# The first output projection of a two-layer decoder kernel, turned from weight blocks to token tiles

## The chip, the cores and the metric

The kernel runs on one core of a Trainium2 chip. The metric is the device time of one execution in microseconds; the median of the runs shown is compared. The engines are named as in the profile: PE (matrix products, with its weight loads as PEld), DVE (vector), ACT (scalar, which also issues the stores), POOL, and SP (which issues the loads).

## The reference

Two layers over 1024 tokens of width 1024, batch 1. Each normalises its input, projects it, mixes tokens (layer A: dilated sliding-window attention in three groups of eight heads, merged per head; layer B: a gated linear recurrence), attends in four more heads to 256 memory rows, gates and projects back:

```python
h = rms_norm(x, norm_gain[l])
cols = h @ w_in                        # mixer | memory queries | gate
y = concat(mix, mem_out) * silu(gate)  # width 1024 + 512
x = x + y @ w_out                      # 1536 x 1024
```

The change concerns the last line of layer A and what stands before and after it.

## The kernel before

All matrix products keep single precision by splitting each operand into a high part and a remainder, and adding three products (high x high, high x remainder, remainder x high). A weight piece is 256 x 512 numbers, stored as 128 rows of 1024. `piece` (L189) loads it into one of two `raw` buffers (SP, L195), copies the high part `wh` (ACT, L166) and subtracts to get `wl` (DVE, L210). The pieces stand in one list in order of use; `take` (L233) hands out the next ones and `ahead(n)` (L227) makes sure that the next n are under way. They live in a ring of four slots (`wring`), which `more_weights` (L182) widens for a stretch by slots on the right-hand side of on-chip memory.

`project_tiles` (L256) takes four pieces, a 1024 x 512 block of weights, and goes over the eight token tiles of 128 in pairs. A pair sums into two of the three PSUM banks named `acc`, 2 x 24 matmuls of 128 x 512, and `each(m, ps)` empties a bank. The normalised input stands transposed and split on chip (`hhi`, `hlo`).

Layer A ends so. For the last head group the keys, values and queries are projected (L927 to L930). Each query tile goes through a norm, a rotary turn on POOL, a transposition, and `attend` (L834) for the tile before: scores, softmax, product with the values, and `merge` (L813), which reads the other two groups' outputs from DRAM into the two `os` buffers of the pool `gs` (`fetch_group`, L808), scales and adds them (L827, L830) and stores the tile to `o_scr`. The eighth tile's `attend` is called inside the last gate chunk (`gate_chunk`, L500), after its first pair of token tiles (L513). That chunk is the second half of the mixer's gate: per tile a tanh on ACT (L497), a product on DVE (L498) and a store to `gate_scr` (L512). Tiles 0 to 3 are written into the heads' `qn` buffers (`room`, L505), the others into `os`.

Then `out_proj` (L561) does the projection with `load_a` to `finish_a` (L949 to L982). Its steps run over three blocks `b0` of 512 rows of `w_out` (8: the memory heads, 0 and 4: the two halves of the mixer), and inside each over eight token tiles. A step loads a mixed slice and its gate (`ol`, `gt`, three buffers each, L955 or L957 and L958), multiplies them (L967), brings the product into transposed, split form (for b0 = 8 by a copy and a subtraction, L971 and L972; otherwise through four transpositions on PE, L291), and adds 2 x 12 matmuls (L609 to L611) into a pair of `acc` banks, which DVE adds to the input row `x1` (L616). Loads are issued three steps ahead and products made two steps ahead (`LEAD`). All eight `x1` tiles stay on chip. In the last block each tile is finished: stored, normalised (`norm_rows`, L272) and, one step later, transposed into the next layer's `hhi`, `hlo` (`put_hT`, L454). The weights come through the ring, widened by `W_OA` = 3 to seven slots. The first projection of layer B (L1002) follows.

What the program writes is not the order in which an engine works. The tile framework plans each engine's order ahead of the run, with expected times; what is written earlier goes first if it is ready. The engines then work through their planned order, and a buffer, on chip or in PSUM, passes to its next user when the last one is done with it. Pools that are closed give their memory to the pools opened next.

Of the kernel before, what the change touches and what calls it, by code (L numbers as in the profile page):

```python
# [30 lines left out]
D = 1024  # L31
# [16 lines left out]
LEAD = 2  # L48
# [2 lines left out]
ZR = 4  # L51
ZQ = 2
WR = 4
W_A, W_OA, W_B, W_OB = 1, 3, 2, 2
XL = 1
SQB = 1
MGP = ((0,),(1,),(),())
# [60 lines left out]
def trunk_kernel(ctx, tc, x, mem, pos, norm_gain, w_in_a, q_gain_a, k_gain_a, qk_gain_t, w_out_a,  # L118
# [58 lines left out]


    plan, ready = [], {}
    more, turn = [], [0]  # L180

    def more_weights(stack, n=2, start=0):  # L182

# [5 lines left out]
    def piece(src, gain=None):  # L189


        a = src.shape[1]
        raw = rpool.tile([128, 1024], F32, name="raw")
        v = lambda t: t.rearrange("p (a b) -> p a b", a=a)
        WQ.dma_start(v(raw[:]), src)  # L195
        pool = wpool
        if more:
# [12 lines left out]
        W_LO.tensor_tensor(lo[:], raw[:], hi[:].bitcast(F32), op=OP.subtract)  # L210
        return v(hi[:]), v(lo[:])
# [41 lines left out]
            if after:  # L253
                after(i)

    def project_tiles(key, lhs, each, order=None):  # L256

        W = take(key, 4)
        for m0 in range(0, NT, 2):
            pss = [pp.tile([128, 512], F32, name="acc") for _ in range(2)]  # L260
            project([ps[:] for ps in pss], [lhs(m0), lhs(m0 + 1)], W,
                    (lambda i: ahead(3 + i)) if m0 == NT - 2 else None, order)
            if m0 == 0:
                ahead(2)
            for i, ps in enumerate(pss):
                each(m0 + i, ps[:])
# [2 lines left out]
        copy(e_hi, hi, ps)  # L269
        V.tensor_sub(lo, ps, hi.bitcast(F32))  # L270

    def norm_rows(xt, gain, n, pool, parts=1):  # L272

        xn = pool.tile([128, D], F32, name="xn", bufs=2)
        ss = small.tile([128, 1], F32, name="ss1")
        A.activation(xn[:], xt, AF.Square, accum_out=ss[:])
        r = rsqrt(ss[:], 1, D)
        w = n // parts
        if gain is None:
            V.tensor_scalar(xn[:], xt, r[:], None, op0=OP.mult)  # L280
            return xn
        for c in (slice(i * w, (i + 1) * w) for i in range(parts)):
            V.scalar_tensor_tensor(xn[:, c], xt[:, c], r[:], gain[:, c], op0=OP.mult, op1=OP.mult)
        return xn
# [212 lines left out]
        A.activation(dst, src, AF.Tanh, scale=0.5)  # L497
        V.scalar_tensor_tensor(dst, dst, 1.0, src, op0=OP.add, op1=OP.mult)  # L498

    def gate_chunk(c, by_residue, between=None, room=None):  # L500

        def each(m, ps):
            pool, name = room if room and m < 4 else (gs, "os")  # L505
            sg = pool.tile([128, 4, 128], F32, name=name)[:].rearrange("p h d -> p (h d)")
            twice_silu(sg, ps)
            scr = gate_scr[:, c * 512:(c + 1) * 512]
# [3 lines left out]
                SQ.dma_start(sequence_rows(scr, m), sg)  # L512
            if between and m == 1:  # L513
                between()

        project_tiles(("gate", c), lhs_natural, each)

    def feature_proj(key, halves=lambda t, hf: t[:, hf * 512:(hf + 1) * 512]):

# [41 lines left out]
    def out_proj(key, load, load_x, y_T, x1, finish, pool, before):  # L561

        steps = [(b0, m) for b0 in FIRST for m in range(NT)]
        loaded, made, W = {}, {}, {}

        def weights(b0):
            p = take((key, b0), 4)
            W[b0] = [p[0:2], p[2:4]]  # L570

        def fetch(i):
            if i < len(steps):
                loaded[i], last = load(steps[i][1], steps[i][0])
                if XL <= i < NT + XL:
                    with tc.issue_after(last.ins):
                        load_x(i - XL)

        def make(i):
            if i < len(steps):  # L580
# [2 lines left out]
                y_T(steps[i][1], steps[i][0], loaded.pop(i), hi, lo)  # L583
                made[i] = hi, lo

        for i in range(LEAD + 1):
            fetch(i)
        for i in range(LEAD):
            make(i)
        before()  # L590
        later = None
        for i, (b0, m) in enumerate(steps):
            if m == 0:
                weights(b0)
            fetch(i + LEAD + 1)
            make(i + LEAD)
            if later:
                later()
                later = None
            hi, lo = made.pop(i)  # L600
            if m == 1:
                ahead(2)
            pss = [pp.tile([128, 512], F32, name="acc") for _ in range(2)]
            last = i == len(steps) - 1 and key == "out_b"
            for kp, ch in ((0, 0), (1, 0), (0, 1), (1, 1)) if last else ((0, 0), (0, 1), (1, 0), (1, 1)):
                wh, wl = W[b0][kp][ch]
                for j in range(2):
                    k = 2 * kp + j
                    T.matmul(pss[ch][:], hi[:, k, :], wh[:, j, :], start=k == 0, stop=False)  # L609
                    T.matmul(pss[ch][:], hi[:, k, :], wl[:, j, :], start=False, stop=False)  # L610
                    T.matmul(pss[ch][:], lo[:, k, :], wh[:, j, :], start=False, stop=k == 3)  # L611
                if m == NT - 1:
                    ahead(3 + 2 * kp + ch)
            for ch, ps in enumerate(pss):
                xs = x1[m][:, ch * 512:(ch + 1) * 512]
                V.tensor_tensor(xs, xs, ps[:], op=OP.add)  # L616
            if b0 == FIRST[-1]:
                later = finish(m)
        if later:
            later()  # L620


    gate_order = (8, 9), (10, 11, 0, 1, 2, 3, 4), (5, 6, 7)
# [47 lines left out]
    plan_out("out_b", w_out_b)  # L671

    wide = ExitStack()


    with ExitStack() as sa:
# [107 lines left out]
        with ExitStack() as s1:  # L784
# [103 lines left out]
            for Q, g in group_order:  # L888
# [39 lines left out]
                project_tiles(("v", Q, g), lhs, each_v, order)  # L928
                waiting = []
                project_tiles(("q", Q, g), lhs, each_q, order)  # L930
                last = lambda: attend(Q, g, *waiting.pop(), kT, kl, vv)
                if (Q, g) == group_order[-1]:
                    wide.close()
                    gate_chunk(1, False, last, (ap_, "qn"))
                else:
                    last()

    with ExitStack() as s2:  # L940
        more_weights(s2, W_OA, at_piece[1] - at_piece[0])
        op = s2.enter_context(tc.tile_pool(name="outp", bufs=1))
        x1 = op.tile([128, NT, D], F32, name="x1")
        x1 = [x1[:, m, :] for m in range(NT)]
        gainb = op.tile([128, D], F32, name="gainb")
        row_bcast(gainb[:], norm_gain[1], D)
        hnew = []

        def load_a(m, b0):  # L949
            r = slice(m * 128, (m + 1) * 128)  # L950
            o = op.tile([128, 512], F32, name="ol", bufs=3)
            gt = op.tile([128, 512], F32, name="gt", bufs=3)
            if b0 == 8:
                for t, scr in ((o, om_scr), (gt, gatem_scr)):
                    last = LQ.dma_start(t[:].rearrange("p (k t) -> p k t", k=4), scr[:, r].rearrange("(k p) t -> p k t", p=128))  # L955
            else:
                LQ.dma_start(o[:], o_scr[r, 0, b0 * 128:b0 * 128 + 512])  # L957
                last = LQ.dma_start(gt[:], gate_scr[r, b0 * 128:b0 * 128 + 512])  # L958
            return (o, gt), last

        def load_x(m):
            LQ.dma_start(x1[m], x[m * 128:(m + 1) * 128, :])

        def y_a(m, b0, loaded, hi, lo):
            o, gt = loaded
            y = o[:]
            V.tensor_tensor(y, y, gt[:], op=OP.mult)  # L967
            if b0 == 8:
                y = y.rearrange("p (k r j) -> p k j r", k=4, r=4)
                hi, lo = (t[:].rearrange("p k (j r) -> p k j r", r=4) for t in (hi, lo))  # L970
                copy(A, hi, y)  # L971
                V.tensor_sub(lo, y, hi.bitcast(F32))  # L972
                return
            transposed_split(y, hi, lo, 4)

        def finish_a(m):
            if not hnew:
                hnew.append(1)
                new_hT()
            xn = norm_rows(x1[m], gainb[:], D, op, 2 if m == NT - 1 else 1)  # L980
            SQ.dma_start(x1_scr[m * 128:(m + 1) * 128, :], x1[m])
            return lambda: put_hT(xn, m)  # L982

        out_proj("out_a", load_a, load_x, y_a, x1, finish_a, op, lambda: None)


    with ExitStack() as sb:
        more_weights(wide, W_B)
# [257 lines left out]
        with ExitStack() as s7:  # L1246
# [45 lines left out]
            out_proj("out_b", load_b, load_x, y_b, x1, finish_b, op, last_gates)  # L1292


# [40 lines left out]
```

## Time and profile before

| what | us |
|---|---|
| median of 3 runs (2157.15 to 2159.2) | 2158.18 |
| the profiled execution | 2157.36 |
| its span, first to last instruction | 2155.2 |
| PE busy | 2134.3 |
| DVE busy | 1079.5 |
| ACT busy | 729.8 |

Times in the views are from the start of the span. The chain of waits names who waited, for whom, in total, how often, and the longest; an entry in brackets in the timeline is idle time just before the instruction and what ended it. A row of a timeline gives start, length, engine, line, operation, output and inputs; an engine's name with a q is its queue issuing a transfer.

### The profile page before, as it was taken

What the parts mean: (1) busy time and instruction counts of PE and PEld (TensorE: products, weight loads), DVE (VectorE), ACT (ScalarE), POOL (GpSimd) and SP (SyncE); (2) the same over time, 40 slices, a digit from 0 to 9 for tenths busy, and PEclk for the clock granted to TensorE, in tenths of its full rate; (3) what the DMA queues carried; (4) which work ended last, traced back from release to release, by engine and by line L of the source; (5) the groups of instructions that cost most, each with busy time, mean ns of one, the idle gap of its engine ahead of it and who ended that gap; (6) DMA issues with size and microseconds to landing.
All of it is one profiled execution on the core that took longest, in us unless ns stands there. A gap on an engine that the chain in (4) does not pass through costs nothing.

```text
span 2155.2 us, 29643 instructions
## 1 busy us (share of the span) xinstructions
PE 2134.3 (99%) x11273; PEld 1813.5 (84%) x11273; DVE 1079.5 (50%) x2435; ACT 729.8 (34%) x1507; POOL 370.9 (17%) x600
## 2 busy tenths in 40 slices
PE   8999999999999999999999999999999999999999
PEld 6888888888888888888888877778888888888887
DVE  6755323324414324425834755634657772776443
ACT  4545323324423324323423521333532221232211
POOL 1013212312403302312222100012200000000221
PEclk9999999999999999999999999999999999999999
DMA  6543211221121121111311474420301112113633
GB/s 200 135 144 66 53 44 53 62 59 49 51 77 50 43 62 47 50 57 52 114 54 55 129 263 147 146 83 25 115 28 55 59 55 59 49 54 94 234 120 114
DMA packets 181004, 183.49 MB, mean 85 GB/s; under 512 B 49008, under 2 KB 117760, under 8 KB 180864
## 3 DMA queue, kind: packets, MB, share of 16 engines
q1 hardware_dynamic: 116592, 138.48, 21.2%
q10 hardware_dynamic: 64272, 43.13, 7.0%
q8 instruction: 89, 1.46, 0.3%
q14 instruction: 51, 0.42, 0.1%
HBM read 138.45 MB, written 43.12 MB: 84 GB/s over the span
## 4 chain that ended last, share of the span: by engine, by line
PE 95%; DMA 2%; DVE 1%; ACT 1%; issue 0%; SPq 0%; POOL 0%; ACTq 0%; DVEq 0%
PE acc L250 17%; PE acc L251 17%; PE acc L252 17%; PE acc L527 5%; PE acc L528 5%; PE acc L529 5%; PE acc L609 4%; PE acc L611 4%; PE acc L610 4%; PE po L877 3%; PE pt L308 2%; PE s L858 2%; PE s L1091 1%; PE pt L1091 1%; PE pt L871 1%; PE pt L291 1%
## 5 line engine op out<-in xcount | busy, mean ns | idle before, releaser
L250 PE MATMUL acc<-wh,hhi 128*128 128x512 f32 x1440 | 564.3, 395 | 2.4 <-ACT vb L166 1.2
L251 PE MATMUL acc<-wl,hhi 128*128 128x512 f32 x1440 | 566.1, 394 | 0.0
L252 PE MATMUL acc<-wh,hlo 128*128 128x512 f32 x1440 | 566.1, 395 | 0.0
L175 POOL TENSOR_TENSOR rr<-rv,nhalf 128x4 f32<-128x4 f32 (+1 forms) x150 | 147.5, 983 | 1374.3 <-DVE rv L173 1360.3
L210 DVE TENSOR_TENSOR wl<-raw,wh 128x1024 fp32r<-128x1024 f32 x152 | 189.0, 1244 | 368.0 <-ACT wh L166 365.9
L250 PEld LDWEIGHTS acc<-wh,hhi 128*128 128x128 f32 x1440 | 271.3, 188 | 56.0 <-ACT vb L166 1.4
L251 PEld LDWEIGHTS acc<-wl,hhi 128*128 128x128 f32 x1440 | 271.2, 188 | 53.2 <-DVE wl L210 0.4
L252 PEld LDWEIGHTS acc<-wh,hlo 128*128 128x128 f32 x1440 | 270.9, 188 | 53.0
L166 ACT ACTIVATE wh<-raw 128x1024 fp32r<-128x1024 f32 x152 | 160.7, 1059 | 186.1 <-PE acc L252 63.2
L529 PE MATMUL acc<-hhi,wl 128*128 128x512 f32 x512 | 204.1, 399 | 0.0
L528 PE MATMUL acc<-hlo,wh 128*128 128x512 f32 x512 | 203.8, 398 | 0.0
L527 PE MATMUL acc<-hhi,wh 128*128 128x512 f32 x512 | 203.0, 396 | 0.0
L609 PE MATMUL acc<-wh,yhi 128*128 128x512 f32 x384 | 152.8, 402 | 4.4 <-ACT yhi L166 2.6
L299 DVE TENSOR_REDUCE ss<-sq 128x4 f32<-128x512 f32 x116 | 79.3, 683 | 146.7 <-ACT sq L297 146.5
L610 PE MATMUL acc<-wl,yhi 128*128 128x512 f32 x384 | 151.1, 393 | 0.1
L611 PE MATMUL acc<-wh,ylo 128*128 128x512 f32 x384 | 149.4, 394 | 0.2 <-DVE ylo L972 0.2
L297 ACT ACTIVATE sq<-acc 128x512 f32<-128x512 f32 x116 | 68.9, 594 | 183.6 <-PE acc L252 179.5
L302 DVE TENSOR_TENSOR qn<-acc,rr 128x512 f32<-128x512 f32 x116 | 79.6, 688 | 92.9 <-PE pt L308 50.6
L866 ACT ACTIVATE pa<-pa,st 128x128 f32<-128x128 f32 (+1 forms) x192 | 84.4, 441 | 100.1 <-DVE st L864 96.0
L528 PEld LDWEIGHTS acc<-hlo,wh 128*128 128x128 f32 x512 | 96.4, 188 | 17.9
L527 PEld LDWEIGHTS acc<-hhi,wh 128*128 128x128 f32 x512 | 96.4, 188 | 17.6
L529 PEld LDWEIGHTS acc<-hhi,wl 128*128 128x128 f32 x512 | 96.4, 188 | 17.5
(233 smaller groups left out, 3191.7 us busy)
## 6 DMA issues: line engine op xcount, KB each, us to landing
raw<-in_w_in_a_dram SPq DMA_DIRECT2D x88, 512.0 KB
raw<-in_w_in_b_dram SPq DMA_DIRECT2D x40, 512.0 KB
o_scr<-os ACTq DMA_DIRECT2D x48, 256.0 KB
raw<-in_w_mem_kv_dram SPq DMA_DIRECT2D x16, 512.0 KB
os<-o_scr SPq DMA_DIRECT2D x32, 256.0 KB
raw<-in_w_out_a_dram SPq DMA_DIRECT2D x12, 512.0 KB
raw<-in_w_out_b_dram SPq DMA_DIRECT2D x12, 512.0 KB
gt<-gateb_scr SPq DMA_DIRECT2D x24, 256.0 KB
```

What stands on the lines that cost most here:

```text
L166: A.activation(dst, src, AF.Copy)
L175: G.tensor_tensor(r[:], v[:], nhalf[:, :n], op=OP.pow)
L210: W_LO.tensor_tensor(lo[:], raw[:], hi[:].bitcast(F32), op=OP.subtract)
L250: T.matmul(ps, hi, wh[:, j, :], start=at == 0, stop=False)
L251: T.matmul(ps, hi, wl[:, j, :], start=False, stop=False)
L252: T.matmul(ps, lo, wh[:, j, :], start=False, stop=at == n - 1)
L527: T.matmul(to, wh[:, k, :], mh, start=k == 0, stop=False)
L528: T.matmul(to, wh[:, k, :], ml, start=False, stop=False)
L529: T.matmul(to, wl[:, k, :], mh, start=False, stop=k == 7)
L609: T.matmul(pss[ch][:], hi[:, k, :], wh[:, j, :], start=k == 0, stop=False)
L610: T.matmul(pss[ch][:], hi[:, k, :], wl[:, j, :], start=False, stop=False)
L611: T.matmul(pss[ch][:], lo[:, k, :], wh[:, j, :], start=False, stop=k == 3)
```

## The change

**The order of the projection.** The steps run over token tiles, and inside a tile over the three blocks. The sum over all 1536 rows stays in one pair of `acc` banks, emptied once for each tile instead of three times. Each tile is finished at its third step.

```diff
-        steps = [(b0, m) for b0 in FIRST for m in range(NT)]
+        steps = [(b0, m) for m in range(NT) for b0 in FIRST] if by_tile else [(b0, m) for b0 in FIRST for m in range(NT)]
...
+                first, end = (b0 == FIRST[0], b0 == FIRST[-1]) if by_tile else (True, True)
+                if first:
+                    pss = [pp.tile([128, 512], F32, name="acc") for _ in range(2)]
...
+                        T.matmul(pss[ch][:], hi[:, k, :], wh[:, j, :], start=first and k == 0, stop=False)
...
+                for ch, ps in enumerate(pss) if end else ():
```

**Weights.** All twelve pieces have a place of their own (`W_OA` = 6): two in the widened ring, three in a pool over the last keys (`wearly`), three in a pool over the heads' buffers (`wlate`), four in the ring. A list `rooms` says which pool each piece goes to, for the first ten pieces of layer B too.

```diff
+        early, late = (s2.enter_context(tc.tile_pool(name=n, bufs=3, side="right")) for n in ("wearly", "wlate"))
+        rooms.extend([more[0]] * W_B + [early] * 3 + [late] * 3 + [wpool] * WR)
+        rooms.extend([more[0]] * W_B + [wpool] * WR + [more[0]] * W_B + [wpool] * (WR - W_B))
```

**When.** The pools are opened inside the last gate chunk, right after the eighth tile's `attend`, where those of the heads are closed. From gate tile 2 on the pieces are asked for two more at a tile, up to eight; the rest follow in the last pair. In that pair, after its first weight piece, the loads and products of the first two projection steps are made (`begin`); the rest of the projection (`rest`) comes after the chunk.

```diff
+            if between and m > 1:
+                ahead(min(W_OA + W_B, 2 * m - 2))
...
+                    def between():
+                        last()
+                        s1.close()
+                        sa.close()
+                        out_a.append(begin_out_a(s2))
+
+                    def to_out(i):
+                        if i == 0:
+                            out_a[0][0]()
+                        ahead(W_OA + W_B + 1 + i)
+
+                    gate_chunk(1, False, between, (ap_, "qn"), to_out)
```

**What pays for the memory.** The ring has four slots instead of five from the last queries on (`wide.close()` moves ahead of them, and `ahead` there asks for no more than four). `x1` has two buffers instead of eight tiles, `xn` one instead of two, `ol` two instead of three, and `gt` uses the two `os` buffers instead of three of its own. Gate tiles 2 and 3 go to `os` as well.

```diff
-            pool, name = room if room and m < 4 else (gs, "os")
+            pool, name = room if room and m < 2 else (gs, "os")
...
-            o = op.tile([128, 512], F32, name="ol", bufs=3)
-            gt = op.tile([128, 512], F32, name="gt", bufs=3)
+            o = op.tile([128, 512], F32, name="ol", bufs=2)
+            gt = gs.tile([128, 4, 128], F32, name="os")[:].rearrange("p h d -> p (h d)")
```

The load of `x1` for a tile is issued behind the loads of its third step. The second output projection (layer B) keeps its order.

More of the change, by code (lines that the diff above doesn't have):

```diff
@@ L179, in trunk_kernel @@
     plan, ready = [], {}
-    more, turn = [], [0]
+    more, turn, rooms = [], [0], []
     def more_weights(stack, n=2, start=0):
@@ L196, in piece @@
         pool = wpool
-        if more:
+        if rooms:
+            pool = rooms.pop(0)
+        elif more:
             if turn[0] >= WR:
@@ L254, in project, with project_tiles @@
                 after(i)
-    def project_tiles(key, lhs, each, order=None):
+    def project_tiles(key, lhs, each, order=None, end=None):
         W = take(key, 4)
@@ L261, in project_tiles @@
             project([ps[:] for ps in pss], [lhs(m0), lhs(m0 + 1)], W,
-                    (lambda i: ahead(3 + i)) if m0 == NT - 2 else None, order)
-            if m0 == 0:
+                    (end or (lambda i: ahead(3 + i))) if m0 == NT - 2 else None, order)
+            if m0 == 0 and not end:
                 ahead(2)
@@ L498, in twice_silu, with gate_chunk @@
         V.scalar_tensor_tensor(dst, dst, 1.0, src, op0=OP.add, op1=OP.mult)
-    def gate_chunk(c, by_residue, between=None, room=None):
+    def gate_chunk(c, by_residue, between=None, room=None, end=None):
         def each(m, ps):
-            pool, name = room if room and m < 4 else (gs, "os")
+            pool, name = room if room and m < 2 else (gs, "os")
             sg = pool.tile([128, 4, 128], F32, name=name)[:].rearrange("p h d -> p (h d)")
@@ L514, in each @@
                 between()
-        project_tiles(("gate", c), lhs_natural, each)
+            if between and m > 1:
+                ahead(min(W_OA + W_B, 2 * m - 2))
+        project_tiles(("gate", c), lhs_natural, each, end=end)
     def feature_proj(key, halves=lambda t, hf: t[:, hf * 512:(hf + 1) * 512]):
@@ L574, in fetch @@
                 loaded[i], last = load(steps[i][1], steps[i][0])
-                if XL <= i < NT + XL:
+                xm = i // 3 if by_tile and i % 3 == 2 else i - XL if not by_tile and XL <= i < NT + XL else None
+                if xm is not None:
                     with tc.issue_after(last.ins):
-                        load_x(i - XL)
+                        load_x(xm)
         def make(i):
@@ L584, in make, with begin @@
                 made[i] = hi, lo
[L586 to L596, printed above, removed]
+        def begin():
+            for i in range(LEAD):
+                fetch(i)
+            for i in range(LEAD):
+                make(i)
+            before()
@@ new lines, in rest @@
+        def rest():
+            fetch(LEAD)
+            later = None
+            for i, (b0, m) in enumerate(steps):
+                if m == 0:
+                    weights(b0)
+                fetch(i + LEAD + 1)
+                make(i + LEAD)
+                if later:
+                    later()
+                    later = None
+                hi, lo = made.pop(i)
+                if m == 1 and not by_tile:
+                    ahead(2)
+                first, end = (b0 == FIRST[0], b0 == FIRST[-1]) if by_tile else (True, True)
+                if first:
+                    pss = [pp.tile([128, 512], F32, name="acc") for _ in range(2)]
+                last = i == len(steps) - 1 and key == "out_b"
+                for kp, ch in ((0, 0), (1, 0), (0, 1), (1, 1)) if last else ((0, 0), (0, 1), (1, 0), (1, 1)):
+                    wh, wl = W[b0][kp][ch]
+                    for j in range(2):
+                        k = 2 * kp + j
+                        T.matmul(pss[ch][:], hi[:, k, :], wh[:, j, :], start=first and k == 0, stop=False)
+                        T.matmul(pss[ch][:], hi[:, k, :], wl[:, j, :], start=False, stop=False)
+                        T.matmul(pss[ch][:], lo[:, k, :], wh[:, j, :], start=False, stop=end and k == 3)
+                    if m == NT - 1:
+                        ahead(min(4, 2 + 2 * kp + ch) if by_tile else 3 + 2 * kp + ch)
+                for ch, ps in enumerate(pss) if end else ():
+                    xs = x1[m][:, ch * 512:(ch + 1) * 512]
+                    V.tensor_tensor(xs, xs, ps[:], op=OP.add)
+                if b0 == FIRST[-1]:
+                    later = finish(m)
@@ L597, in out_proj @@
             if later:
                 later()
[L599 to L620, printed above, removed]
+        return begin, rest
     gate_order = (8, 9), (10, 11, 0, 1, 2, 3, 4), (5, 6, 7)
@@ L927, in trunk_kernel @@
                 project_tiles(("k", Q, g), lhs, each_k, order)
[L928 removed]
+                final = (Q, g) == group_order[-1]
+                end = (lambda i: ahead(min(3 + i, WR))) if final else None
+                project_tiles(("v", Q, g), lhs, each_v, order, end)
                 waiting = []
[L930 removed]
+                if final:
+                    wide.close()
+                project_tiles(("q", Q, g), lhs, each_q, order, end)
@@ L935, in trunk_kernel @@
                 else:
                     last()
[L940 to L950, printed above, removed]
-            o = op.tile([128, 512], F32, name="ol", bufs=3)
-            gt = op.tile([128, 512], F32, name="gt", bufs=3)
[L953 to L984, printed above, removed]
@@ L987, in trunk_kernel @@
+    with s2:
+        out_a[0][1]()
     with ExitStack() as sb:
-        more_weights(wide, W_B)
         bk = sb.enter_context(tc.tile_pool(name="bk", bufs=1))
@@ L1290, in finish_b @@
                     SQ.dma_start(out[m * 128:(m + 1) * 128, c], x1[m][:, c])
-            out_proj("out_b", load_b, load_x, y_b, x1, finish_b, op, last_gates)
+            for part in out_proj("out_b", load_b, load_x, y_b, x1, finish_b, op, last_gates):
+                part()
 _OUTS = [((1, S, D), 'float32')]
```

52 lines of the change are left out of this document (45 added, 7 removed).

## The prediction

> **What bounds the kernel now.** I read the page first, then the tensor engine's waits, then the work by stretch of time around the first output projection, and last the timeline there.
>
> ```profile
> span 2155.2 us, 29643 instructions
> PE 2134.3 (99%) x11273; PEld 1813.5 (84%) x11273; DVE 1079.5 (50%) x2435; ACT 729.8 (34%) x1507; POOL 370.9 (17%) x600
> ```
> ```profile
> PE pt L291 <- DVE xn L283: 8.1, 1, 8.1
> PE acc L609 <- ACT yhi L166: 2.6, 3, 1.9
> PE acc L609 <- DVE x L616: 1.6, 2, 1.0
> PE acc L250 <- ACT vb L166: 1.2, 1, 1.2
> ```
> ```profile
> 1196.80:1246.00 49.20, 49.20 (x312) 44.15 (x312) 34.95 (x126) 19.29 (x66) 6.10 (x10) 1.00 0.45 132
> 1246.00:1260.60 14.60, 14.60 (x65) 11.76 (x64) 3.60 (x11) 3.40 (x7) 0.00 (x0) 1.00 0.60 172
> 1260.60:1407.20 146.60, 141.80 (x655) 114.30 (x655) 94.40 (x130) 44.79 (x60) 3.31 (x6) 0.99 0.55 182
> 1407.20:1440.00 32.80, 31.62 (x154) 26.05 (x153) 15.60 (x22) 12.81 (x21) 4.88 (x5) 1.00 0.40 126
> ```
>
> The tensor engine (PE) is the bound everywhere: it is busy for 99% of the span. So a change that keeps every matmul can only win the time in which PE stands or runs slowly. The waits say where it stands: 8.1 us at the very start of the kernel, which the change does not touch, and 2.6 + 1.6 + 1.2 us that all lie in the stage at hand. In the table of stretches (columns: length, then busy time and count for PE, weight loads, DVE, ACT, POOL; PE clock; DMA share; GB/s) the first two rows are the tail of the attention with the last gate chunk: PE has no idle time at all. The third is the output projection: 4.8 us idle out of 146.6. The fourth is the start of the next layer: 1.2 us. The whole prize is therefore a few microseconds in 2155.
>
> ```profile
> 1260.22 0.39 PE L252 MATMUL acc<-wh,hlo 128*128 128x512 f32 x1
> 1262.52 0.55 PE L609 MATMUL acc<-wh,yhi 128*128 128x512 f32 x1 [1.91 <-ACT yhi L166]
> 1265.97 0.53 PE L610 MATMUL acc<-wl,yhi 128*128 128x512 f32 x1
> 1266.34 0.39 PE L611 MATMUL acc<-wh,ylo 128*128 128x512 f32 x1
> 1266.57 0.39 PE L609 MATMUL acc<-wh,yhi 128*128 128x512 f32 x1
> 1323.38 0.50 PE L609 MATMUL acc<-wh,yhi 128*128 128x512 f32 x1 [1.03 <-DVE x L616]
> 1371.23 0.50 PE L609 MATMUL acc<-wh,yhi 128*128 128x512 f32 x1 [0.60 <-DVE x L616]
> 1433.18 0.50 PE L250 MATMUL acc<-wh,hhi 128*128 128x512 f32 x1 [1.18 <-ACT vb L166]
> ```
> ```profile
> 1248.75 3.96 DMA o_scr<-os
> 1253.73 6.66 DMA gt<-gatem_scr
> 1260.57 0.70 DVE ol L967
> 1261.34 1.14 ACT yhi L166
> 1262.50 1.12 DVE ylo L972
> ```
>
> At full rate matmuls start 0.23 us apart (1266.34 to 1266.57). The step from the gate chunk to the projection costs twice: 1262.52 - 1260.22 - 0.23 = 2.1 us of standing, and then eight matmuls (first start 1262.52, last 1265.97) that take 3.8 us up to 1266.34 instead of 8 x 0.23 = 1.8, another 2.0. The chain (second fence) says why: the first loads waited for the memory of the last attention tile (write done 1248.75 + 3.96 = 1252.7), the load took 6.66 us, and the product and its split 0.70 + 1.14 + 1.12.
>
> **The change part by part: what goes.** The first products are made inside the last gate pair and their buffers lie over tables and values that are free sooner, so the 2.1 + 2.0 = 4.1 us can go whole; what can be late instead is priced below. Next, the sum over twelve slices of the mixed width now stays in PSUM: 24 pairs of additions (L616) become 8.
>
> ```profile
> L616 DVE TENSOR_TENSOR x<-x,acc x96: 674/687/708, 1268.0 to 2151.6; 128x512 f32<-128x512 f32 x96
> DVE ol L967 <- DMA ol<-o_scr: 14.7, 11, 2.3
> ```
> That saves DVE 32 x 0.69 = 22 us, of which PE sees nothing except where it waited for such an addition: 1.03 + 0.60 = 1.6 us. A third of the occasions stays, and the cause of the delay, DVE standing in its queue for a load (second row, 11 times, up to 2.3 us), stays with two load buffers where there were three; the splits of weights, which crowded DVE at the same places, leave the stage. I take 1.1 us. The two smaller waits for a split (2.6 - 1.9 = 0.7 us) come where eight norms follow one another in the last third; now one norm falls in each tile: 0.5. The 1.2 us at 1433 come from an eviction queued behind the transposes of the last tiles; seven of eight tiles are now done earlier, but the order there is planned afresh: 0.6, between 0 and 1.2. Matmuls and transposes keep their number. Gains: 4.1 + 1.1 + 0.5 + 0.6 = 6.3 us, at most 4.1 + 1.6 + 0.7 + 1.2 = 7.6.
>
> **What is moved.** Ten of the twelve weight pieces now come before the projection, where two came before (the queue of SP, below); each costs a load, a copy on ACT and a subtraction on DVE.
>
> ```profile
> 1196.27 2.94 SPq L195 DMA_DIRECT2D raw<-in_w_out_a_dram  x2
> 1262.42 0.37 SPq L195 DMA_DIRECT2D raw<-in_w_out_a_dram  x1
> 1357.84 4.22 DMA raw<-in_w_out_a_dram
> L210 DVE TENSOR_TENSOR wl<-raw,wh 128x1024 fp32r<-128x1024 f32 x152 | 189.0, 1244 | 368.0 <-ACT wh L166 365.9
> L166 ACT ACTIVATE wh<-raw 128x1024 fp32r<-128x1024 f32 x152 | 160.7, 1059 | 186.1 <-PE acc L252 63.2
> ```
> Twelve pieces are 12 x 1.24 = 15 us of DVE and 12.7 us of ACT. In the 63.8 us of the first two stretches DVE is free for 25 and ACT for 41, so they fit, and the DMA share there is 0.45 and 0.60. Cost nothing, as long as gate matmuls cover; without that cover a piece costs up to its 4.22 + 1.06 + 1.24 us. The ring of four slots instead of five over the last queries costs nothing either: a slot is freed by the last pair a full pair (48 x 0.23 = 11 us) before its next piece is used.
>
> **What is added: a wait for room.** This is where I chose. Gate tiles 2 and 3 used to be evicted into the heads' `qn` buffers. Those are closed now, so the tiles go to the two `os` buffers, which the last attention tiles hold for their merge.
>
> ```profile
> 1221.42 0.59 ACTq L512 DMA_DIRECT2D gate_scr<-qn  x1
> 1225.90 0.60 ACT L497 ACTIVATE qn<-acc 128x512 f32<-128x512 f32 x1 [6.25 <-DMA gate_scr<-qn]
> 1226.87 0.61 ACT L497 ACTIVATE qn<-acc 128x512 f32<-128x512 f32 x1
> 1236.27 0.57 ACT L497 ACTIVATE qn<-acc 128x512 f32<-128x512 f32 x1
> 1241.49 1.11 SPq L810 DMA_DIRECT2D os<-o_scr  x2
> 1244.14 1.95 PE L877 MATMUL po<-vv,pts 128*128 128x128 f32 x16
> 1246.53 2.19 DVE L830 SCALAR_TENSOR_TENSOR os<-os,mw 128x128 f32<-128x128 f32 x8 [4.27 <-ACT os L827]
> 1248.41 0.60 ACT L497 ACTIVATE os<-acc 128x512 f32<-128x512 f32 x1 [1.14 <-PE acc L252]
> 1249.04 0.69 DVE L498 SCALAR_TENSOR_TENSOR os<-os,acc 128x512 f32<-128x512 f32 x1 [0.32 <-ACT os L497]
> ```
> Before, tiles 2 and 3 left PSUM at 1226.87 and 1236.27. Both `os` buffers are filled for the last attention tile at 1241.49 and given back during its merge: half of 2.19 us after 1246.53, at 1247.6. Until then gate tiles 2 and 3 sit in two of the three `acc` banks and tile 4 in the third. So PE has 5 x 24 = 120 gate matmuls to fill the attention's pauses with. Before, it used 192 - 65 = 127 by 1246.0, (65 from the second stretch's row): it runs dry 7 x 0.23 = 1.6 us early, near 1244.4, and tile 5 can start when tile 2 is evicted, 1247.6 + 0.60 + 0.69 = 1248.9. That is 4.5 us of standing if the attention keeps its pace. It can quicken: the last value product at 1244.14 stood behind gate matmuls, and without them it and the merge come up to 3 us sooner, which leaves 1.5. Bounds: 0 (if the planner finds other work for PE) and 4.5 + 2.0 for slow matmuls after such a pause, as at 1262.52. I take 2.5 of standing, nearer to the quickened case since an idle PE lets the chain run, and 1.0 of slow matmuls, half of what one pause cost: 3.5.
>
> Whether the slow matmuls follow is read from the rows above: 1.91 us of standing brought them, 1.03 and 1.18 did not. The Trainium skill (TensorE: Matmul & The Clock Gate, "Part 1: The HAM clock gate") says that the clock is halved only after an idle window of about 3.4 us. By that rule the tail would cost 2.5 and the time would be 1.0 us lower than below; the trace does not bear it out, since 1.91 us were enough.
>
> Behind that wait stand, on ACT's queue, the later gate evictions, and on SP's the gate loads of the projection, which use the same two buffers: 0.5 us for a late start of the first tile, between 0 and what the second rival gives.
>
> **Sum.** -6.3 + 3.5 + 0.5 = -2.3 us. The profiled execution took 2157.36 us, 2.16 outside its span; that is 0.8 below the median of 2158.18, so I take the difference from the median: 2155.9 us. About 0.2% (4.3 us) is what a measurement of this kernel can tell from no change, so this forecast reads "no difference", with its own range of 2152 to 2160 from the bounds of the tail (0 to 6.5) and of the gains.
>
> **The rivals.** *The tail stays covered.* The planner places the last attention tile earlier, and all gains come: 2158.2 - 7.6 = 2150.6 us. For it: PE's order is planned against expected times, and the value product stood idle work away from its input. Against: the merge, not PE, holds the buffers.
>
> *The two `os` buffers become the bound, and it gets slower.* Each round through them is an eviction and a write: 0.60 + 0.69 + (1225.90 - 1221.42) = 5.8 us. Tiles 2, 3 and then 4, 5 take two rounds from 1247.6 to 1259.2; only then can the first gate load start, 6.66 us to 1265.9, and product and splits end at 1268.9. With the full tail (6.5) the gate's matmuls end at 1260.6 + 6.5 = 1267.1, so PE stands 1.8 us again and runs slowly for 2.0; tiles 6 and 7 then hold up the loads of the third and fourth step for about 3 more. -6.3 + 6.5 + 3.8 + 3 = +7: 2165.2 us. It decides when the first gate load lands after the last gate matmul. For it: every duration is from a row. Against: the planner knows these buffers and can send gate loads earlier.
>
> *The pieces are not on chip in time*, so the change does not do what it says. Seven of the twelve come late: three lie over the last attention tile's memory, free at 1252.7, and four in the gate's own slots, which its last pair frees. With two loads in flight 7 x 4.22 / 2 = 15 us, done by 1267.5; one at a time 29.5 us, by 1282.2. The last piece is used in the last quarter of the third step: the gate ends at 1260.6 + 3.5 = 1264.1, two steps of 24 matmuls are 11 us, three quarters of a step 4.1, so it is due at 1279.2. PE waits 0 to 3 us for the load and 2.3 more for its split: up to 2155.9 + 5.3 = 2161.2 us.
>
> **How the numbers follow.** Forecast 0.46, covered tail 0.24, buffers as the bound 0.20, late pieces 0.10. The forecast's range reaches past -4.3 us with 0.13 of its 0.46; of the second case 0.22 lie beyond, of the last two 0.22 lie above +4.3. Faster 0.35, no difference 0.43, slower 0.22. The range for 8 in 10 runs from just under the covered tail, 2150, to near the slow end, 2164.
>
> **What would show it.** Right: no L609 matmul waits 2 us at the gate's end; PE waits between about 1244 and 1249 for a gate eviction (L497) that waited for an `os` buffer; waits for L616 under 1 us; no weight load of this projection after its first step. Wrong: PE without a pause before the projection (then first rival), a new wait for `yhi` at its start with gate loads landing late (second), or for a weight split (third).

## The result, and the profile after

The kernel became slower: 2168.0 us, median of 5 runs (2166.3 to 2171.9), against 2158.18 us (2157.2 to 2159.6) of 5 runs of the kernel before beside them. The ratio is 1.0047, with a 95% interval of 1.0032 to 1.0061: 9.8 us more, where 2.3 us less was forecast. The prediction was wrong in sign and its range, 2150 to 2164, missed the time. The profiled execution took 2171.9 us, the longest of its five; its span is 14.1 us longer than the one profiled before, so a view of it shows about 4 us more loss than the medians.

The head of the page of the changed kernel, and then its longest waits of the tensor engine (total, times, longest):

```profile
span 2169.3 us, 29613 instructions
PE 2136.6 (98%) x11273; PEld 1816.0 (84%) x11273; DVE 1059.1 (49%) x2403; ACT 730.5 (34%) x1507; POOL 370.9 (17%) x600
```
```profile
PE pt L294 <- DVE xn L286: 8.6, 1, 8.6
PE acc L252 <- DVE os L501: 8.6, 1, 8.6
PE acc L622 <- ACT yhi L166: 4.5, 3, 2.6
PE pt L294 <- DVE ol L724: 3.0, 2, 2.1
PE acc L622 <- DVE os L501: 1.2, 1, 1.2
```

PE has as many matmuls as before. DVE lost 20 us of work (32 instructions fewer, as counted), which is worth nothing by itself. The first wait is the start of the kernel, as before. The second is new: one pause of 8.6 us, for a gate eviction (L501) into `os`. The last three all lie at the start of the projection, where the kernel before had one wait of 1.91 us. The waits for the additions to `x1` and for the next layer's `vb` no longer appear.

Where in time? The same three stretches, first of the kernel before, then of the changed one (length, busy time and count of PE, weight loads, DVE, ACT, POOL; PE clock; DMA share; GB/s). 1244.3 is where PE's first pause begins in the changed kernel.

```profile
1244.30:1303.00 58.70, 56.61 (x252) 45.94 (x251) 33.11 (x49) 16.27 (x20) 0.00 (x0) 0.97 0.76 252
1303.00:1410.00 107.00, 104.29 (x497) 84.12 (x496) 65.66 (x93) 31.91 (x47) 3.31 (x6) 1.00 0.44 143
1410.00:1440.00 30.00, 28.82 (x141) 23.76 (x140) 14.82 (x20) 12.81 (x21) 4.88 (x5) 1.00 0.39 120
```
```profile
1244.30:1303.00 58.70, 41.13 (x153) 31.49 (x154) 25.50 (x37) 16.65 (x23) 0.00 (x0) 0.85 0.67 211
1303.00:1410.00 107.00, 107.00 (x520) 89.02 (x519) 48.97 (x71) 27.27 (x42) 3.74 (x6) 1.00 0.46 147
1410.00:1440.00 30.00, 30.00 (x146) 25.02 (x145) 15.65 (x20) 11.67 (x16) 1.10 (x2) 1.00 0.41 126
```

From 1303 on the changed kernel is better: PE never stands, 2.7 + 1.2 = 3.9 us won. All that is lost is lost in the 58.7 us before, where PE stands for 17.6 us at a clock of 0.85. The order by token tiles itself is no loss; its beginning is.

The timeline around the pause. The last value product (PE, L945) ended at 1244.3; SP rows are issues of loads, L878 the merge's, L898 the merge's arithmetic, L166 and L212 the copy and the subtraction of a weight piece, L500 and L501 the two steps of a gate eviction. (The merge's output, first operand of L898, is an `os` of another pool with the same name.)

```profile
1241.36 0.34 SPq L878 DMA_DIRECT2D os<-o_scr  x1
1242.21 1.06 ACT L166 ACTIVATE wh<-raw 128x1024 fp32r<-128x1024 f32 x1 [2.85 <-DMA raw<-in_w_out_a_dram]
1243.30 1.23 DVE L212 TENSOR_TENSOR wl<-raw,wh 128x1024 fp32r<-128x1024 f32 x1 [1.62 <-ACT wh L166]
1244.44 0.61 DVE L898 SCALAR_TENSOR_TENSOR os<-os,mw 128x128 f32<-128x128 f32 x2
1245.32 0.34 SPq L878 DMA_DIRECT2D os<-o_scr  x1
1248.67 1.06 ACT L166 ACTIVATE wh<-raw 128x1024 fp32r<-128x1024 f32 x1 [1.75 <-DMA raw<-in_w_out_a_dram]
1249.63 0.58 ACT L500 ACTIVATE os<-acc 128x512 f32<-128x512 f32 x1
1249.96 1.14 DVE L898 SCALAR_TENSOR_TENSOR os<-os,mw 128x128 f32<-128x128 f32 x4 [2.64 <-DMA os<-o_scr]
1251.02 1.22 DVE L212 TENSOR_TENSOR wl<-raw,wh 128x1024 fp32r<-128x1024 f32 x1
1252.15 1.28 DVE L501 SCALAR_TENSOR_TENSOR os<-os,acc 128x512 f32<-128x512 f32 x2
1252.89 0.80 PE L252 MATMUL acc<-wh,hhi 128*128 128x512 f32 x1 [8.60 <-DVE os L501]
```

Read it upwards from PE. It waited for the last step of gate tile 2 (L501, 1252.15). That step stood on DVE's queue behind the subtraction of a weight piece (L212, 1251.02), and that behind the second half of the merge (L898, 1249.96). This half waited for its load, which was issued at 1245.32, not with the other one at 1241.36 (before, both went out together at 1241.49). It was issued late because its `os` buffer was still in use by the tile before, whose last two operations ran at 1244.44: they stood on DVE's queue behind the subtraction of a piece (1243.30), and that behind a copy on ACT which waited 2.85 us for the piece's load.

Tile 2 itself did not need that second buffer. The first half of the merge, four operations from 1246.18 to 1247.32, had given back the other `os`, into which tile 2 goes: its first step (L500, 1249.63) began before the second half did. This step too stood behind a piece, a copy on ACT (1248.67) that waited 1.75 us for its load. So tile 2's wait for room ended at 1247.3, and the rest of the pause is time in queues: weight pieces that nobody needed yet stood ahead of the merge and of the eviction for which PE waited.

The start of the projection, from the same timeline: L711 is the first load of a gate slice, L724 the product, L294 a transpose for it, L622 to L624 matmuls of the projection.

```profile
1265.87 1.06 ACT L166 ACTIVATE wh<-raw 128x1024 fp32r<-128x1024 f32 x1 [5.96 <-DMA raw<-in_w_out_a_dram]
1266.83 0.58 ACT L500 ACTIVATE os<-acc 128x512 f32<-128x512 f32 x1
1268.55 0.37 SPq L711 DMA_DIRECT2D os<-gatem_scr  x1
1271.49 0.69 DVE L724 TENSOR_TENSOR ol<-ol,os 128x512 f32<-128x512 f32 x1 [2.70 <-DMA os<-gatem_scr]
1273.41 0.50 PE L622 MATMUL acc<-wh,yhi 128*128 128x512 f32 x1 [2.56 <-ACT yhi L166]
1278.50 0.66 PE L294 MATMUL pt<-ident,ol 128*128 128x128 f32 x4 [2.10 <-DVE ol L724]
1281.11 0.79 PE L622 MATMUL acc<-wh,yhi 128*128 128x512 f32 x1 [1.18 <-DVE os L501]
1281.70 0.63 PE L623 MATMUL acc<-wl,yhi 128*128 128x512 f32 x1
1282.13 0.63 PE L624 MATMUL acc<-wh,ylo 128*128 128x512 f32 x1
1296.69 0.80 PE L622 MATMUL acc<-wh,yhi 128*128 128x512 f32 x1 [1.23 <-ACT yhi L166]
```

The slice was loaded at 1268.55, where it had been meant to lie ready: its buffer is an `os` too, and gate tiles passed through both. The matmuls at 1281.70 and 1282.13 are 0.43 us apart instead of 0.23: the clock has dropped. The wait at 1281.11 is for a PSUM bank that one of the last two gate tiles still held. Pieces stand in the queues here as well: tile 5's first step (L500, 1266.83) came behind a copy that had waited 5.96 us for its load. So these first steps hold the shared buffers and the pieces together.

And the chain that ended last shows the round through an `os` buffer which the later steps wait for:

```profile
1282.28 7.78 DMA gate_scr<-os
1290.07 4.61 DMA os<-gatem_scr
1294.77 0.70 DVE ol L724
1295.55 1.10 ACT yhi L166
```

A gate tile is written (7.78 us), only then is the next slice loaded into its buffer (4.61), then product and split, and PE begins at 1296.69.

The sum closes to 1 us. Standing: 8.60 at the tail; 2.56 + 0.38 + 2.10 + 1.18 + 0.85 + 0.69 + 1.23 = 8.99 in the projection's first steps. Slow matmuls, each stretch's length less 0.227 us for each of its matmuls: 1.4 after 1252.89, 2.6 after 1281.11, 1.5 after 1296.69. Together 23.1. Before paid 4.1 at this place, and 3.9 are won later: 23.1 - 4.1 - 3.9 = 15.1 us, against 14.1 between the two spans.

### The profile page after: what moved, and what is told of

Same layout as the page of the kernel before. It is cut to its first block, busy times and chain, and to the rows that moved or that the text cites. A ratio compares the mean times of both kernels' runs of the same rounds, so it can differ in the third digit from the quotient of the medians.

```text
span 2169.3 us, 29613 instructions
## 1 busy us (share of the span) xinstructions
PE 2136.6 (98%) x11273; PEld 1816.0 (84%) x11273; DVE 1059.1 (49%) x2403; ACT 730.5 (34%) x1507; POOL 370.9 (17%) x600
## 4 chain that ended last, share of the span: by engine, by line
PE 95%; DMA 3%; DVE 1%; ACT 1%; issue 0%; POOL 0%; SPq 0%; ACTq 0%; DVEq 0%
PE acc L252 16%; PE acc L253 16%; PE acc L254 16%; PE acc L532 5%; PE acc L533 5%; PE acc L534 5%; PE acc L624 4%; PE acc L622 4%; PE acc L623 4%; PE po L945 2%; PE pt L311 2%; PE s L926 2%; PE s L1128 1%; PE pt L1128 1%; PE pt L939 1%; DMA raw<-in_w_out_a_dram 1%
## 5 line engine op out<-in xcount | busy, mean ns | idle before, releaser
L212 DVE TENSOR_TENSOR wl<-raw,wh 128x1024 fp32r<-128x1024 f32 x152 | 187.9, 1238 | 383.5 <-ACT wh L166 381.0
L166 ACT ACTIVATE wh<-raw 128x1024 fp32r<-128x1024 f32 x152 | 160.8, 1059 | 189.8 <-PE acc L254 57.3
L622 PE MATMUL acc<-wh,yhi 128*128 128x512 f32 x384 | 153.8, 403 | 5.7 <-ACT yhi L166 4.5
L624 PE MATMUL acc<-wh,ylo 128*128 128x512 f32 x384 | 150.2, 397 | 0.4 <-DVE ylo L729 0.4
L534 PEld LDWEIGHTS acc<-hhi,wl 128*128 128x128 f32 x512 | 96.3, 188 | 17.6
L532 PEld LDWEIGHTS acc<-hhi,wh 128*128 128x128 f32 x512 | 96.3, 188 | 17.6
```

The lines of the kernel that those rows point to most:

```text
L166: A.activation(dst, src, AF.Copy)
L532: T.matmul(to, wh[:, k, :], mh, start=k == 0, stop=False)
L534: T.matmul(to, wl[:, k, :], mh, start=False, stop=k == 7)
L622: T.matmul(pss[ch][:], hi[:, k, :], wh[:, j, :], start=first and k == 0, stop=False)
```

## The experiments

Three theories. R: the room. Gate tiles 2 and 3, and then 4 to 7 and the slices, have only the two `os` buffers. S: weight pieces, asked for early, stand on ACT's and DVE's in-order queues ahead of the merge and the evictions. T, the rival of both: the projection by tiles is slow by itself.

**Other room for tiles 2 and 3.** They go into the projection's `x1` buffers, which are not in use yet.

```diff
-            sg = pool.tile([128, 4, 128], F32, name=name)[:].rearrange("p h d -> p (h d)")
+            if room and 2 <= m < 4:
+                sg = gate_room[0]()
+            else:
+                sg = pool.tile([128, 4, 128], F32, name=name)[:].rearrange("p h d -> p (h d)")
...
+        gate_room.append(lambda: op.tile([128, D], F32, name="x1", bufs=2)[:, 0:512])
```

> The changed kernel, with gate tiles 2 and 3 evicted into the two x1 buffers of the projection (laid over the rotary tables, free before) instead of the two os buffers. Theory R (the tensor engine stands because gate tiles 2 and 3 wait for the os buffers of the last merge): the pause of 8.6 us after 1244 and the slow matmuls behind it (about 1.3 us) go, the waits at the start of the projection stay or shrink: 2154 to 2160 us. Theory S (the weight pieces, queued on ACT and DVE ahead of the merge while their loads land late, make the pause): the last merge still ends near 1251, and later than in the kernel before. Theory T (the order by tiles with two load buffers is itself slower): most of the loss stays, 2164 us or more.

Measured: 2169.5 us, ratio 1.0053 (1.0040 to 1.0065). The pause stayed, 8.08 us. Its timeline:

```profile
1252.90 0.80 PE L252 MATMUL acc<-wh,hhi 128*128 128x512 f32 x1 [8.08 <-DVE os L501]
1256.13 1.08 ACT L500 ACTIVATE x<-acc 128x512 f32<-128x512 f32 x2 [5.87 <-DMA o_scr<-os]
```

The tiles meant for `x1` could only go there at 1256.13, after the write of the last attention tile. The pool's memory lies over that tile's, so the other room wasn't there when it was needed. The experiment missed its aim: it says nothing against R.

**Only the room, in the kernel before.** Nothing of the change but this one digit:

```diff
-            pool, name = room if room and m < 4 else (gs, "os")
+            pool, name = room if room and m < 2 else (gs, "os")
```

> The kernel before, with one edit: gate tiles 2 and 3 go to the os buffers instead of the heads' qn buffers. R: a pause of the tensor engine in the gate chunk of 2.5 to 4.5 us, with up to 2 us of slow matmuls: 2161 to 2165 us. S: little of the pause without the early pieces, under 2 us: 2158 to 2160. A pause of 8 us or more here would say that the early pieces have no part in it: 2167 or more.

Measured: 2162.89 us (11 runs), ratio 1.0023 (1.0014 to 1.0032), 4.9 us slower. In its timeline both merge loads go out together, and the pause is 3.51 us:

```profile
1242.66 1.11 SPq L810 DMA_DIRECT2D os<-o_scr  x2
1247.80 0.60 ACT L497 ACTIVATE os<-acc 128x512 f32<-128x512 f32 x1 [0.96 <-DVE os L830]
1249.17 0.80 PE L250 MATMUL acc<-wh,hhi 128*128 128x512 f32 x1 [3.51 <-DVE os L498]
```

R holds in mechanism, but it is not the whole 8.6 us. (The 4.9 us are not the price of this pause alone: its profile also shows slow matmuls, and a wait of 3.22 us for a weight split at 1274, which the changed kernel doesn't have.)

**No early request for the pieces.** The `ahead(...)` at the gate tiles is left out.

```diff
-            if between and m > 1:
-                ahead(min(W_OA + W_B, 2 * m - 2))
```

> The changed kernel without the requests for pieces at gate tiles 2 to 7; all twelve are asked for from the last gate pair on. R alone: the pause in the gate chunk stays at 8 us. R with S: it shrinks to the 2.5 to 4.5 us that the wait for the os buffers costs by itself; but the pieces then come late for the projection and cost up to as much there: 2164 to 2172 us in all, with the loss moved behind the gate chunk.

Measured: 2168.67 us, ratio 1.0050 (1.0037 to 1.0062).

```profile
1252.60 0.79 PE L252 MATMUL acc<-wh,hhi 128*128 128x512 f32 x1 [8.58 <-DVE os L501]
```

The pause stayed because the planner set the pieces at the same times although they were asked for later: the subtractions stand where they stood. So this was no test of S.

**All gate tiles from 2 on into `x1`.** As the first experiment, with `2 <= m < 8`.

> The changed kernel with all gate tiles from 2 on in the x1 buffers, so that after the last merge the os buffers carry only the projection's own gate slices. R: the pause in the gate chunk and most of the waits in the first four steps go, the gains of the order by tiles stay (about 7 us against the kernel before): 2150 to 2154 us. T: the waits in the first steps stay, 2158 or more.

Measured: 2169.49 us, ratio 1.0058 (1.0045 to 1.0070).

```profile
1257.73 0.80 PE L252 MATMUL acc<-wh,hhi 128*128 128x512 f32 x1 [12.73 <-DVE x L501]
```

The pause grew to 12.73 us, for the reason of the first experiment: no gate tile from 2 on had room until 1256, none of them went to `os`. But behind it the waits of the projection shrank to 3.82 and 1.68 us, since the slices had both `os` buffers to themselves. One loss was traded for the other.

**The pieces' loads behind the merge's.** The last ten pieces are loaded only after the last attention tile's second merge load has been issued.

```diff
+        if hold and 2 <= held[0] < 12:
+            with tc.issue_after(hold[0].ins):
+                WQ.dma_start(v(raw[:]), src)
+        else:
+            WQ.dma_start(v(raw[:]), src)
+        held[0] += len(hold)
...
+                if (Q, m) == (1, NT - 1):
+                    hold[:] = [d]
```

> The changed kernel, with the loads of the last ten weight pieces queued behind the last two loads for the merge (the planner had placed two of them ahead, whatever the place of the request). If the early pieces lengthen the pause (theory S on top of R), the merge ends near 1248 instead of 1251 and the pause falls from 8.6 to 3.5 us, as in the kernel before with the os buffers alone; the pieces come later for the projection and may take some of it back: 2161 to 2167 us. If S is wrong the pause stays at 8 us: 2167 or more.

Measured: 2169.05 us, ratio 1.0046 (1.0032 to 1.0060). The merge is early now, but the pause is still 7.73 us:

```profile
1245.54 2.37 DVE L907 SCALAR_TENSOR_TENSOR os<-os,mw 128x128 f32<-128x128 f32 x8 [2.53 <-ACT os L904]
1249.87 1.06 ACT L166 ACTIVATE wh<-raw 128x1024 fp32r<-128x1024 f32 x1 [3.58 <-DMA raw<-in_w_out_a_dram]
1250.83 1.07 ACT L507 ACTIVATE os<-acc 128x512 f32<-128x512 f32 x2
1252.83 0.80 PE L259 MATMUL acc<-wh,hhi 128*128 128x512 f32 x1 [7.73 <-DVE os L508]
```

The merge ends at 1247.9 and the buffers are free. But the next thing on ACT's queue is the copy of a piece, whose load it awaits until 1249.87; the eviction (L507) stands behind it. The pieces had only moved their place in the queue. By its expectation this pause would speak against S; the timeline shows that pieces were still ahead of the eviction, so it decides nothing.

**The pieces' loads behind the gain's.** The same hold, now behind the load of the norm's gain, which waits for the last attention tile's memory. In the order of instructions no piece stands any more among the merge and the first three evictions.

```diff
-        row_bcast(gainb[:], norm_gain[1], D)
+        hold.append(row_bcast(gainb[:], norm_gain[1], D))
```

> The changed kernel with one difference: the loads of the last ten weight pieces stand on SP's queue behind the load of the gain of the norm, which waits for the last attention tile's memory (about 1256). By the orders of instructions, no piece then stands on DVE or ACT among the merge of the last attention tile and the first three gate evictions, which the earlier hold (behind the merge's loads) had not reached. R with S (the room itself costs 3.5 us, and the rest of the 8.6 us pause comes from pieces queued ahead of the merge and the evictions): the second merge load issues near 1242 instead of 1245.32, the merge ends near 1248, gate tile 2 leaves its bank near 1249.5, and PE's pause at the gate's end is 3 to 4.5 us as in the kernel before with only the rooms changed (3.51). Rival (the pieces in the queues are chance; the tail without matmuls of tiles 2 and 3 is slow by itself in this order): the pause stays at 7.5 to 9 us. Either way the pieces come later, from about 1256 on, seven or more of them with 4 to 7 us a load, so PE should wait for weight splits in the first steps of the projection, and the total is no test: 2163 to 2178.

Measured: 2169.06 us, ratio 1.0053 (1.0036 to 1.0070); and this is the tail:

```profile
1241.42 1.19 SPq L885 DMA_DIRECT2D os<-o_scr  x2
1246.24 1.66 DVE L905 SCALAR_TENSOR_TENSOR os<-os,mw 128x128 f32<-128x128 f32 x6 [0.84 <-DMA os<-o_scr]
1247.42 0.60 ACT L507 ACTIVATE os<-acc 128x512 f32<-128x512 f32 x1 [1.89 <-DVE os L905]
1248.79 0.80 PE L259 MATMUL acc<-wh,hhi 128*128 128x512 f32 x1 [4.44 <-DVE os L508]
```

Both merge loads go out together again, the eviction follows the merge at once, and the pause is 4.44 us instead of 8.60. With the pieces out of the queues, what is left is R alone. So S is shown for 4.2 us of the pause, by one profiled execution of each kernel. The total did not move: the pieces come later, and PE waits 2.61, 1.12, 2.70 and 2.71 us in the projection's first steps, with slow matmuls.

**Room that is really free.** `x1` and the gain get a pool of their own, opened first so that it lies over memory that is free earlier, and all gate tiles from 2 on go there. The mixed slices (`ol`) get a second pool.

```diff
+            if room and 2 <= m < 8:
+                sg = gate_room[0]()
...
+        xp = s2.enter_context(tc.tile_pool(name="outx", bufs=1))
+        lp_ = s2.enter_context(tc.tile_pool(name="outl", bufs=2))
...
+        gate_room.append(lambda: xp.tile([128, D], F32, name="x1", bufs=2)[:, 0:512])
-        gainb = op.tile([128, D], F32, name="gainb")
+        gainb = xp.tile([128, D], F32, name="gainb")
...
-            o = op.tile([128, 512], F32, name="ol", bufs=2)
+            o = lp_.tile([128, 512], F32, name="ol")
...
-            x1[m] = op.tile([128, D], F32, name="x1", bufs=2)[:]
+            x1[m] = xp.tile([128, D], F32, name="x1", bufs=2)[:]
```

> As the run with all gate tiles in the x1 buffers, but these buffers in a pool of their own over the rotary tables alone, so that they come free with the last scores (1236) and not with the last attention tile's store (1256). R: gate tiles 2 and 3 leave PSUM near 1236, no pause before 1250 though the merge stays late; the gains of the order by tiles stay: 2149 to 2156 us. If the pause comes from the late merge and not from the rooms, it stays at 8 us: 2165 or more. T: waits in the first four steps of 5 us or more, 2158 to 2163.

Measured: 2153.5 us (11 runs), ratio 0.9979 (0.9970 to 0.9988): faster than both kernels. Tiles 2 and 3 leave PSUM at 1236 and PE has no pause in the gate chunk; the stretch from 1244.3 on, at full clock, is the third row here:

```profile
1235.23 0.33 SPq L162 DMA_DIRECT2D gainb<-in_norm_gain_dram  x1
1236.20 1.05 ACT L500 ACTIVATE x<-acc 128x512 f32<-128x512 f32 x2
```
```profile
1244.30:1303.00 58.70, 52.98 (x245) 41.85 (x245) 32.05 (x47) 21.44 (x30) 0.56 (x1) 1.00 0.79 258
```

The gain's load, which shares the pool, could be issued at 1235.23 instead of 1256.17: that is the room which the change lacked. The edit changes rooms only: for the gate tiles, for the gain and `x1`, and for `ol`, whose first load goes out at 1249.25 instead of 1256.56. Together they are the 14.5 us between this kernel and the changed one. And T falls as the cause of the loss: the same order by tiles, with the same pieces, beats the order before. Something of T's sign is left: PE still stands 58.70 - 52.98 = 5.7 us in this stretch, 3.04 of them in one wait for a product at 1260.23.

**The same, tiles 2 and 3 alone.** `2 <= m < 4`, so that tiles 4 to 7 share `os` with the slices.

> The same with only gate tiles 2 and 3 in the x1 buffers; tiles 4 to 7 share the os buffers with the projection's first gate slices. R: no pause in the gate chunk, but the first gate slices wait behind the stores of tiles 4 to 7: 3 to 6 us slower than with all tiles in the x1 buffers, 2153 to 2161 us.

Measured: 2162.94 us (11 runs), ratio 1.0018 (1.0010 to 1.0027). No pause in the gate chunk, but the projection starts late:

```profile
1259.78 0.36 SPq L717 DMA_DIRECT2D os<-gatem_scr  x1
1265.49 0.79 PE L625 MATMUL acc<-wh,yhi 128*128 128x512 f32 x1 [4.73 <-ACT yhi L166]
```

In the kernel with all the tiles in the new pool this slice was loaded at 1251.05. So the two halves of R are apart. The new pools with room for tiles 2 and 3 are worth 2168.0 - 2162.9 = 5 us, and room for tiles 4 to 7 on top of them another 9.4, where 3 to 6 were expected.

**The new pool with the first hold.** All tiles in it, and the last ten pieces behind the merge's loads.

> All gate tiles in the x1 buffers' own pool, and the last ten pieces queued behind the merge's loads. No pause in the gate chunk in either theory; against the run without the hold the merge ends earlier, but the pieces come later: within 3 us of it, 2149 to 2157 us.

Measured: 2153.39 us (8 runs), ratio 0.9976 (0.9966 to 0.9986), the same as without the hold. Where nobody waits for the merge's buffers, pieces ahead of it cost nothing that can be measured.

## Why the prediction was wrong

**The later gains came, and larger than taken.** Waits for additions and splits, and the start of the next layer: 1.1 + 0.5 + 0.6 forecast, at most 1.6 + 0.7 + 1.2 = 3.5; 3.9 came. The sign that went with them, waits for L616 under 1 us, came true.

**What failed first is the price of the wait for room: "I take 2.5 of standing, nearer to the quickened case ... and 1.0 of slow matmuls".** The mechanism, the place and the moment were as forecast: PE ran dry at 1244.3 (forecast 1244.4) and waited for a gate eviction into `os`. It stood 8.6 us and lost 1.4 more in slow matmuls, 10.0 where 3.5 was taken and 6.5 was the bound. Two errors lie in it. The unquickened working, the first `os` free at 1247.6, tile 2 out at 1248.9 and 4.5 us of standing, was the better value: the buffer was free at 1247.3, and with the pieces out of the way PE went on at 1248.79 after 4.44. (In the kernel before with only the rooms changed it stood 3.51.) The value product did come earlier, at 1242.35 instead of 1244.14, and at 1242.41 without the pieces; but there the merge could not follow as far, because it then waited for its load (0.84 us at 1246.24). I had followed one of the merge's two inputs only.

**The second error is the step "Cost nothing, as long as gate matmuls cover"** for the ten pieces. It was a sum of shares: DVE free for 25 us, ACT for 41, so 15 and 12.7 fit. But an in-order queue is not a budget. A copy at the head of ACT's queue, waiting 2.85 us for its load, and a subtraction behind it on DVE delayed two merge operations, and these a load; another copy and another subtraction stood right ahead of the eviction's two steps. All pieces together: 4.2 us, by the two kernels 8.60 - 4.44. The condition that I had named (cover) was missing at just this place, as my own step on the room had worked out; I did not put the two together.

**Third, "0.5 us for a late start of the first tile".** The second rival had this right in mechanism, and its 2165.2 is 2.8 below the measured median. That its number came so near is in part luck: in the profiled execution its losses of 6.5 at the tail and 6.8 at the start were 10.0 and 13.1, and its gains of 6.3 were 4.1 + 3.9 = 8.0, so 15.1 more where it had 7; the medians differ by 9.8. Its condition, that the first gate load lands after the last gate matmul, was met: load issued at 1268.55, product at 1271.49, last gate matmul at 1270.46. The 4.1 us that the change was to win at the transition were lost again there, three times over: PE stood 9.0 us in the first steps and lost 4.1 more in slow matmuls. The rival's sign, a new wait for `yhi` with gate loads landing late, came true with 2.56 us, against the forecast's "no L609 matmul waits 2 us at the gate's end". The kernel with only tiles 2 and 3 in other room shows what the sharing of `os` by tiles 4 to 7 and the slices costs there: 9.4 us. How much of it the pieces in the queues make was not tried. What I held against the rival, "the planner knows these buffers and can send gate loads earlier", has no force: it can order the work, but not make a third buffer. Tiles 2 and 3 and tiles 4 to 7 wait for the same two buffers; I priced the first as likely and small and the second as large and unlikely, where they come together.

**The third rival** (pieces too late) did not decide. In the changed kernel PE waits for no weight split of this projection. The last load of its pieces was issued at 1277.87, ahead of the second half of the first step's 24 matmuls (1281.11 to 1286.40), so the sign "no weight load of this projection after its first step" came true, though only because that step ran so late.

The Trainium skill (TensorE: Matmul & The Clock Gate, "Part 1: The HAM clock gate") says that the window by which the clock is judged runs free, and that the number of slow matmuls varies with its phase at a kernel's start. The runs agree as far as they go: the half clock came in stretches of 3.41 us or a multiple, begun while PE stood or after it had gone on, as the last section shows. Its figure for the idle time that is needed, some 3.4 us, they do not bear out, since 1.91 and 2.61 us were enough.

What stays open: the median of the changed kernel is 3.9 us below its profiled execution, and no trace here shows which of the waits is shorter in the other runs.

## What to carry to other kernels

In these kernels room came free with the memory under its whole pool, as far as the rows show (the gain, `ol` and `x1` of one pool all start at 1256): look for the row of the first operation that uses the pool (here the gain's load, 1256 or 1235), and give buffers that are wanted early a pool over memory that dies early. Work that fits by its share can still stand at the head of an in-order queue with a load it awaits; for every step put ahead of time, ask which buffer the instructions behind it give back, and who waits for that. When two steps of a forecast wait for the same two buffers, price them as one case.

## What the runs showed of the hardware

The length of one pause does not say whether slow matmuls follow. A pause of 1.91 us (the kernel before) and one of 2.61 (the later hold) brought them; 2.56 (the changed kernel) and 3.04 us (the kernel with the new pool) brought none.

The granted clock, read by short stretches, says when it fell. In the kernel before it was at half from 1262.84 to 1266.25. In the changed one it was at half from 1248.90 to 1255.73, from 1279.62 to 1286.45 and from 1296.69 to 1300.10: for 3.41 us or twice that. In the kernel with all gate tiles in `x1` it was 13.66 us, four times that, from 1247.20 on. So the slow matmuls behind a pause are what is left of such a stretch: in the changed kernel it began 4.6 us into the pause of 8.60. And the twelve slow matmuls from 1281.11 on do not come from the pause of 1.18 us just before them: the clock had fallen at 1279.62, before that pause began, and after one of 2.10. A single pause of 1.18 us in the kernel before brought none.

A weight piece's load took 4.22 us at 1357.84 in the kernel before, in a stretch with a DMA share of 0.44. On the chain of the changed kernel such loads took 5.56 us at 1236.63, and 7.31, 6.43 and 3.75 at 1258.54, 1269.02 and 1277.87, in a stretch with 0.67. What makes them so unequal was not tried.
